# A two-layer transformer trunk on one core: stationary tiles placed at multiples of 512 bytes in SBUF

## The chip, the core and the metric

One core of one Trainium2 chip runs the whole program in one launch. The metric is the device time of that launch in microseconds, median of the runs. Before the change it is 2316.6 us (three runs, 2315.55 to 2317.71).

## What is computed

A trunk of two layers over 256 tokens of width 2048, all in fp32. Each layer is a mixer and a squared-ReLU MLP, each behind an RMS norm and added to the residual stream x. Layer 0's mixer joins eight heads of differential attention and eight heads of a gated delta rule; layer 1's is dilated attention over sixteen heads. Most of the arithmetic is the products with weights:

```python
for l in range(DEPTH):                                   # DEPTH = 2
    if l % 2 == 0:
        x = x + diff_delta_mixer(rms_norm(x, ab_norm[i]), ...)   # h @ w_in [2048 x 7184], ..., o @ w_out [2048 x 2048]
    else:
        x = x + dilated_mixer(rms_norm(x, c_norm[i]), ...)       # h @ w_in [2048 x 6144], ..., o @ w_out [2048 x 2048]
    x = x + jnp.square(jax.nn.relu(rms_norm(x, mlp_norm[l]) @ mlp_w1[l])) @ mlp_w2[l]   # 2048 x 8192, 8192 x 2048
```

## The kernel before, in words

**The large products.** `dense` (line 189) makes a block of at most 512 columns of an activation times a weight matrix, for both 128-token halves, in two PSUM tiles. It goes over the contraction in chunks of 128 rows, mostly 16 of them. To keep fp32's accuracy with the faster fp32r matmuls, both operands are split into a high part and a rest: the weights on the fly (ScalarE casts the high part `wh` at line 201, VectorE subtracts it for the rest `wl` at line 107), the activations when they are made. So a chunk is six matmuls of 512 columns, three for each token half: high by high (line 206), high by rest (207), rest by high (208). The activation is the operand that TensorE loads as stationary (128 x 128 fp32, 512 bytes to a partition), the weights are the moving one. Weights come in pieces of two chunks, 512 KB, through four buffers (`wload`, line 174), issued on SyncE's queue; the split goes through six buffers of `wh` and of `wl`.

In this text an intermediate dense product is called by its PSUM tiles: `b`, `bv`, `z`, `a`, `av` make layer 0's inputs, `wo` its output product, `c`, `cv`, `co` the same for layer 1, `m` the MLP's first product and `n` its second. An MLP runs in four groups (`mlp`, line 294); a group is four denses `m_0` to `m_3`, 512 hidden columns each, and four denses `n_0` to `n_3` that take those 2048 hidden columns as their 16 chunks and add to the four column blocks of x. A dense of 16 chunks has 96 matmuls, so a group's `m` half and its `n` half have 384 each, and the program has 9504 such matmuls of 10,230.

**The stationary tiles.** The normed activations of `b` to `a`, `c` and `m` are `xa`, `xb`, `xc`, `xd` (with h or l for the part), in the pool `xp`. The MLP's hidden activations are `hh` and `hl` (in the trace `m_0hh` to `m_3hl`, by their dense), six buffers each in the pools `hp0` and `hp1`. The mixers' outputs `oh` and `ol` (`g0oh` to `g3ol` and `d0oh` to `d3ol` in layer 0, `e0oh` to `e7ol` in layer 1) lie in the mixers' pools `mp` and `mq`, between other tiles. Everything else that is loaded as stationary belongs to small fp32 products and transposes of the mixers and norms: 726 matmuls, of which 420 are transposes.

**From one MLP product to the next.** After the last matmul of a dense `m_b`, ScalarE takes it out of PSUM with the ReLU and squares it (`r`, line 123), VectorE transposes it in 16 instructions of 32 partitions (`hT`, line 289), ScalarE casts the high part (`hh`, line 314) and VectorE subtracts for the rest (`hl`, line 107). That is a generator (`spread`) of which `dense` runs a step every second chunk of the following dense, so VectorE's instructions for it stand between the weight splits of that dense. The hidden block of `m_3` is made within `n_0`, which needs it at its chunks 12 to 15.

**Where a tile lies.** A pool's tiles follow one another in SBUF, and pools follow one another in the order in which they are opened: `cp`, `wp`, `xp`, `sp`, and behind `sp` whatever pool is open at the time (`mp`, then `hp0`, then `mq`, then `hp1`, one after the other over the same place). `sp` holds small scratch tiles and sums to 4736 bytes, which is 9 x 512 + 128. So the pools ahead of it begin at multiples of 512, and each pool behind it begins 128 bytes past one. The built program has the stationary tiles of the 9504 matmuls at these places:

| address modulo 512 | matmuls before | tiles | matmuls after |
|---|---|---|---|
| 0 | 6000 | `xa` to `xd`; `e1` to `e7` of `co` | 9504 |
| 128 | 3072 | all hidden tiles of `n` | 0 |
| 160 | 336 | `d0` to `d3`, `g1` to `g3` of `wo` | 0 |
| 64 | 48 | `g0` of `wo` | 0 |
| 320 | 48 | `e0` of `co` | 0 |

The moving tiles `wh` and `wl` lie at multiples of 512 before and after. Of the 726 small ones 218 lie at a multiple of 512 before and 203 after: most move by 128 bytes, so some come onto a multiple and some leave it.

Of the kernel before, what the change touches and what calls it, by code (L numbers as in the profile page):

```python
# [11 lines left out]
F32 = mybir.dt.float32  # L12
F32R = mybir.dt.float32r
# [4 lines left out]
PSUM = bass.MemoryType.PSUM  # L18

P = 128  # L20
# [67 lines left out]
def trunk(  # L88
# [6 lines left out]

    cp = ctx.enter_context(tc.tile_pool(name="cp", bufs=1))
    wp = ctx.enter_context(tc.tile_pool(name="wp", bufs=6))
    xp = ctx.enter_context(tc.tile_pool(name="xp", bufs=4))
    sp = ctx.enter_context(tc.tile_pool(name="sp", bufs=2))
    dp = ctx.enter_context(tc.tile_pool(name="dp", bufs=1, space=bass.MemoryType.DRAM))  # L100
# [3 lines left out]

# [1 line left out]
    def tt(o, a, b, op):  # L106
# [32 lines left out]
    def rsqrt(o, s, n, scale, name, eps=EPS):  # L139
        """o = (s * scale + eps) ** -0.5, by Newton from the exponent's half."""  # L140
        z = sp.tile([P, 16], F32, tag="rs_z", name=name + "z")[:, :n]
        q = sp.tile([P, 16], F32, tag="rs_q", name=name + "q")[:, :n]
        seed = sp.tile([P, 16], I32, tag="rs_i", name=name + "i")[:, :n]
        ts(z, s, scale, eps, ALU.mult, ALU.add)
        ts(seed, z.bitcast(I32), -0.5, RSQRT_MAGIC, ALU.mult, ALU.add)
        r = seed.bitcast(F32)
        for _ in range(3):
            tt(q, r, r, ALU.mult)
            stt(q, q, -0.5, z, ALU.mult, ALU.mult)
            stt(o, q, 1.5, r, ALU.add, ALU.mult)  # L150
            r = o

    # Work that runs between the steps of the large products: streams of generators.
    streams = {"g": deque(), "s": deque(), "o": deque()}
# [14 lines left out]

# [1 line left out]
    def wload(wsrc, k0, nm):  # L171
# [10 lines left out]
    def drip():  # L182
        """Between two row chunks of a large product: a step of a stream or two."""
        step("gs"[tick[0] % 2])
        if tick[0] % 4 == 3:
            step("o")
        tick[0] += 1

    def dense(wsrc, stat, kcs, nm, pre=(), every=1):
        """[T, sum of columns] = stat.T @ w over the 128-row chunks kcs, in PSUM."""  # L190
        n = sum(s.shape[1] for s in wsrc)
        ps = [psd.tile([P, 512], F32, tag="d", name=f"{nm}p{h}") for h in range(NH)]
        first, last = kcs[0], kcs[-1]
        for j, kc in enumerate(kcs):
            if j % 2 == 0:
                raw = pre[j // 2] if j // 2 < len(pre) else wload(wsrc, kc, nm)
            w = raw[:, j % 2, :n]
            wh = wp.tile([P, 512], F32R, tag="wh", name=f"{nm}h{kc}")[:, :n]
            wl = wp.tile([P, 512], F32R, tag="wl", name=f"{nm}l{kc}")[:, :n]
            with tc.high_priority(offset=AHEAD):  # L200
                S.copy(wh, w)  # L201
                tt(wl, w, wh.bitcast(F32), ALU.subtract)
            for h in range(NH):
                sh, sl = stat(kc, h)
                o = ps[h][:, :n]
                E.matmul(o, lhsT=sh, rhs=wh, start=kc == first, stop=False)  # L206
                E.matmul(o, lhsT=sh, rhs=wl, start=False, stop=False)  # L207
                E.matmul(o, lhsT=sl, rhs=wh, start=False, stop=kc == last)  # L208
            if j % every == 0:
                drip()  # L210
        return ps
# [8 lines left out]

# [1 line left out]
    ca = cp.tile([P, NMAIN], F32, name="ca")  # L222
# [34 lines left out]
    def xt_block(xt, n, norm, nm, dst, pool=None):  # L257
        """Block n of x times the norm's gains, transposed and split, in steps; by the vector engine given a pool."""
        if pool is not None:
# [23 lines left out]
    def turn_quadrant(src, dst, i):  # L283
        """dst[d, chunk, tok] = src[tok, half, (chunk, d)] for the tokens on 32 partitions, by 32x32 blocks."""
        q = slice(32 * i, 32 * i + 32)
        sv = src[q].rearrange("p h (c j f) -> p h c j f", c=4, j=4)
        for j in range(4):
            dv = dst[32 * j:32 * j + 32].rearrange("p c (h t) -> p h c t", h=NH)
            V.transpose(out=dv[:, :, :, q], in_=sv[:, :, :, j, :])  # L289

    def next_norm(n, norm, nm, dst, pool=None):
        """After block n of x is final: what the next norm takes from it."""
        stats_block(xs[n], n, nm + "s")
        yield from xt_block(xs[n], n, norm, nm, dst, pool if n < 3 else None)
        if n == 3:
            stats_end(nm + "e")
            yield
# [38 lines left out]

# [1 line left out]
    win = ab_w_in[0]  # L338
# [6 lines left out]

    grow0 = cp.tile([16, P], F32, name="grow0")
    warm = sp.tile([P, 512], F32, tag="junk", name="warm")
# [6 lines left out]
    for n in range(4):  # L354
# [7 lines left out]
        if n < 3:  # L362
            pre.append(wload(b_cols(0), 2 * n, "b0"))
    with ExitStack() as mix:
        mp = mix.enter_context(tc.tile_pool(name="mp", bufs=1))

# [14 lines left out]

        # rope tables with the gains in them: [tok, half, q/k, dim]
        cga = cp.tile([P, NH, 2, 64], F32, name="cga")
# [66 lines left out]

        # gates and bz
        sz = [None] * NH
# [19 lines left out]
        def gates(a, b):  # L472
            ts(beta, b, 0.5, 0.5, ALU.mult, ALU.add)
            ts(nbeta, beta, -1.0, None, ALU.mult)
            tt(a, a, dtb.unsqueeze(1).broadcast_to([P, NH, 8]), ALU.add)
            # softplus(a) = max(a, 0) + log1p(exp(-|a|)), log1p(y) = 2 atanh(y / (2 + y))
            ab = mp.tile([P, NH, 8], F32, name="gab")
# [55 lines left out]
        def conv(raw, rnm, chunks, y, nm):  # L533
            """y[d, 4, T] = silu(causal conv) of four channel chunks."""
            xc = mp.tile([P, 4, T + 4], F32, tag="xc", name=nm + "x")
# [41 lines left out]
        def gdn(qks, s, vb, nm):  # L577
            """Heads 2s, 2s+1 over both 128-token chunks; tiles are [128, (chunk, head), 128]."""
            def mt(tag, n=4, share=None):
# [23 lines left out]
            ts(sq, rs[:, 4:8], 128.0 ** -0.5, None, ALU.mult)  # L603
            # decays
            dd = mt("dd")
# [23 lines left out]
            for i, (h, e) in enumerate(tiles):  # L629
                hd = 2 * s + e  # L630
                stt(m[:, i, :], pk[:, i * P:(i + 1) * P], nbeta[:, h, hd:hd + 1], dd[:, i, :], ALU.mult, ALU.mult)
            # the 16x16 blocks on m's diagonals, one to a partition
            scr, sxy = scm[s % 2], scx[s % 2]
# [12 lines left out]
            yield  # L646
            # (I + M)^-1 of the blocks, from 2x2 up
            xc = mp.tile([32, 2, BLK, BLK], F32, tag="g_P", name=nm + "xc")
# [30 lines left out]
            for i in range(4):  # L679
                for q in range(2):  # L680
# [3 lines left out]
                        xc[i * 8:(i + 1) * 8, q])  # L684
            # X = (I + M)^-1 and its transpose Y, from those blocks up
            xy = mp.tile([P, 2, 4, P], F32, tag="xy", name=nm + "xy")
# [90 lines left out]
        def out_T(o, nm, dst, s, gain):  # L777
            """dst[s]: [d, head, T], split, of o[tok, (chunk, head), d]."""
            t = ps_t(nm + "ot")
            for h in range(NH):  # L780
                for e in range(2):
                    transpose(t[:, e * T + h * P:e * T + h * P + P], o[:, 2 * h + e, :])
            oh = mp.tile([P, 2, T], F32R, tag=f"oh{nm}", name=nm + "oh")
            ol = mp.tile([P, 2, T], F32R, tag=f"ol{nm}", name=nm + "ol")
            act(oh, quads(t, 2), AF.Identity, scale=gain)
            stt(ol, quads(t, 2), gain, oh.bitcast(F32), ALU.mult, ALU.subtract)
            dst[s] = (oh, ol)
# [35 lines left out]
        def rope_mix(r, dim, cg, sg, h, uw):  # L823
            """uw[:, 0] = the gained and rotated 512 columns (q's and k's) of r[:, h]."""
            hd = dim // 2
# [175 lines left out]

# [1 line left out]
    cb = []  # L1003
    with tc.tile_pool(name="hp0", bufs=6) as hp:
        mlp(0, nb, hp, lambda n: streams["s"].append(next_norm(n, 2, f"xc{n}", cb, hp)))

# [1 line left out]
    cin = c_w_in[0]  # L1008
    cstat = stat_of(cb)
    with ExitStack() as mix:  # L1010
        mp1 = mix.enter_context(tc.tile_pool(name="mq", bufs=1))
        oc = [None] * 8
        vcs = [None] * 4

        def c_side(r, s, nm):
# [55 lines left out]
            for e in range(2):  # L1071
# [3 lines left out]
                E.matmul(po[:, e * T + P:(e + 1) * T], lhsT=vs[1], rhs=pT[:, e, T:], start=False, stop=True)  # L1075
            oh = mp1.tile([P, 2, T], F32R, tag=f"oh{nm}", name=nm + "oh")
            ol = mp1.tile([P, 2, T], F32R, tag=f"ol{nm}", name=nm + "ol")
            S.copy(oh, quads(po, 2))
# [50 lines left out]

# [1 line left out]
    ov = out[0].rearrange("(h p) d -> p h d", p=P)  # L1131
# [32 lines left out]
```

## Time and profile before

| | |
|---|---|
| median of three runs | 2316.6 us |
| span of the profiled execution, first to last instruction | 2313.0 us |
| its time beside the span | 3.6 us less than the median of the runs; the page gives no other time of its own |
| TensorE matmul busy | 2298.6 us of the span |
| TensorE weight load busy | 1889.0 us |
| VectorE / ScalarE busy | 1733.1 / 1275.1 us |
| bytes moved | 426.65 MB, mean 184 GB/s |

How to read it: a matmul's record is longer than its share of the engine, since matmuls are pipelined: one of 512 columns is recorded with some 390 ns, and the next starts some 230 ns after it. So TensorE's pace is read from the starts of matmuls, or from the length of a stretch over the matmuls in it. A weight load is a record of its own (PEld) and stands beside the matmul before it.

### The profile page before, as it was taken

How to read it: one execution, taken by the hardware profiler on the slowest of the kernel's cores; microseconds unless marked ns; L12 is line 12 of the kernel's file. 1: busy time of each engine (PE TensorE's matmuls, PEld its weight loads, DVE VectorE, ACT ScalarE, POOL GpSimd, SP SyncE). 2: the span in 40 equal slices, each digit the busy share in tenths (PEclk: the TensorE clock that was granted, in tenths of full speed). 3: DMA queues.
4: the chain of work that ended last, by engine and by line, in shares of the span. 5: the costliest groups of instructions: out<-in, count | busy, mean ns of one | idle time of the engine just before them, and what ended most of it. 6: DMA issues, size and time to landing. Idle time of an engine off the chain costs nothing.

```text
span 2313.0 us, 31488 instructions
## 1 busy us (share of the span) xinstructions
PE 2298.6 (99%) x10536; PEld 1889.0 (82%) x10536; DVE 1733.1 (75%) x3539; ACT 1275.1 (55%) x2376; POOL 5.6 (0%) x15
## 2 busy tenths in 40 slices
PE   9999999999999999999999999999999999999999
PEld 8888888788888888888888888888888888888887
DVE  7758778867757757857898888987875775775774
ACT  6656665655545545545555555556554554554553
POOL 0000000000000000000000000000000000000000
PEclk9999999999999999999999999999999999999999
DMA  8655454556566666665656555555656656656564
GB/s 264 174 170 166 149 174 143 166 180 190 192 188 183 202 186 186 202 188 186 198 183 200 172 166 176 171 175 181 190 193 189 192 191 190 192 191 189 185 209 155
DMA packets 264775, 426.65 MB, mean 184 GB/s; under 512 B 22514, under 2 KB 94372, under 8 KB 264612
## 3 DMA queue, kind: packets, MB, share of 16 engines
q1 hardware_dynamic: 255812, 420.04, 57.7%
q10 hardware_dynamic: 8800, 4.60, 0.8%
q8 instruction: 82, 1.34, 0.2%
q14 instruction: 81, 0.66, 0.1%
HBM read 420.11 MB, written 4.46 MB: 184 GB/s over the span
## 4 chain that ended last, share of the span: by engine, by line
PE 88%; DVE 8%; DMA 2%; ACT 1%; issue 1%; SPq 0%; ACTq 0%; DVEq 0%
PE n_0p L208 3%; PE n_2p L207 3%; PE n_1p L207 3%; PE n_1p L208 3%; PE n_2p L206 3%; PE n_1p L206 3%; PE n_2p L208 3%; PE n_0p L207 3%; PE n_0p L206 3%; PE n_3p L208 3%; PE n_3p L207 3%; PE n_3p L206 3%; PE m_0p L206 3%; PE m_0p L207 3%; PE m_0p L208 3%; PE m_3p L208 3%
## 5 line engine op out<-in xcount | busy, mean ns | idle before, releaser
L107 DVE TENSOR_TENSOR n_3l<-n_3r,n_3h 128x512 fp32r<-128x512 f32 x128 | 88.5, 692 | 73.0 <-ACT n_3h L201 72.6
L107 DVE TENSOR_TENSOR n_2l<-n_2r,n_2h 128x512 fp32r<-128x512 f32 x128 | 88.4, 692 | 73.0 <-ACT n_2h L201 72.6
L107 DVE TENSOR_TENSOR m_0l<-m_0r,m_0h 128x512 fp32r<-128x512 f32 x128 | 88.5, 692 | 68.0 <-ACT m_0h L201 67.8
L201 ACT CAST n_3h<-n_3r 128x512 fp32r<-128x512 f32 x128 | 79.3, 621 | 94.8 <-PE n_3p L208 59.4
L201 ACT CAST n_2h<-n_2r 128x512 fp32r<-128x512 f32 x128 | 79.3, 620 | 94.8 <-PE n_2p L208 59.4
L107 DVE TENSOR_TENSOR n_1l<-n_1r,n_1h 128x512 fp32r<-128x512 f32 x128 | 87.0, 691 | 55.0 <-ACT n_1h L201 54.8
L201 ACT CAST m_0h<-m_0r 128x512 fp32r<-128x512 f32 x128 | 79.6, 622 | 83.8 <-DVE m_0l L107 39.8
L201 ACT CAST n_1h<-n_1r 128x512 fp32r<-128x512 f32 x128 | 78.6, 620 | 81.7 <-PE n_1p L208 59.4
L201 ACT CAST m_1h<-m_1r 128x512 fp32r<-128x512 f32 x128 | 78.1, 622 | 64.7 <-PE m_1p L208 35.3
L107 DVE TENSOR_TENSOR m_1l<-m_1r,m_1h 128x512 fp32r<-128x512 f32 x128 | 87.1, 691 | 33.7 <-ACT m_1h L201 32.0
L201 ACT CAST n_0h<-n_0r 128x512 fp32r<-128x512 f32 x128 | 77.4, 619 | 48.5 <-PE n_0p L208 37.1
L201 ACT CAST m_3h<-m_3r 128x512 fp32r<-128x512 f32 x128 | 77.1, 621 | 46.8 <-PE m_3p L208 35.3
L201 ACT CAST m_2h<-m_2r 128x512 fp32r<-128x512 f32 x128 | 76.9, 621 | 46.8 <-PE m_2p L208 35.3
L107 DVE TENSOR_TENSOR n_0l<-n_0r,n_0h 128x512 fp32r<-128x512 f32 x128 | 84.9, 689 | 11.3 <-ACT n_0h L201 9.6
L107 DVE TENSOR_TENSOR m_3l<-m_3r,m_3h 128x512 fp32r<-128x512 f32 x128 | 84.9, 689 | 11.3 <-ACT m_3h L201 9.6
L107 DVE TENSOR_TENSOR m_2l<-m_2r,m_2h 128x512 fp32r<-128x512 f32 x128 | 84.9, 689 | 11.2 <-ACT m_2h L201 9.5
L289 DVE STREAM_TRANSPOSE m_0hT<-m_0r 32x256 f32<-32x256 f32 x128 | 55.8, 436 | 10.5 <-ACT m_0r L123 8.0
L289 DVE STREAM_TRANSPOSE m_1hT<-m_1r 32x256 f32<-32x256 f32 x128 | 55.8, 436 | 10.4 <-ACT m_1r L123 7.9
L289 DVE STREAM_TRANSPOSE m_2hT<-m_2r 32x256 f32<-32x256 f32 x128 | 55.8, 436 | 10.4 <-ACT m_2r L123 7.9
L289 DVE STREAM_TRANSPOSE m_3hT<-m_3r 32x256 f32<-32x256 f32 x128 | 55.8, 436 | 10.4 <-ACT m_3r L123 7.9
L208 PE MATMUL n_0p<-n_0h,m_3hl 128*128 128x512 f32 x64 | 25.8, 403 | 0.0
L207 PE MATMUL n_0p<-n_0l,m_2hh 128*128 128x512 f32 x64 | 25.3, 396 | 0.0
(2552 smaller groups left out, 7405.7 us busy)
## 6 DMA issues: line engine op xcount, KB each, us to landing
m_0r<-in_mlp_w_dram SPq DMA_DIRECT2D x64, 512.0 KB
m_1r<-in_mlp_w_dram SPq DMA_DIRECT2D x64, 512.0 KB
m_2r<-in_mlp_w_dram SPq DMA_DIRECT2D x64, 512.0 KB
m_3r<-in_mlp_w_dram SPq DMA_DIRECT2D x64, 512.0 KB
n_0r<-in_mlp_w_dram SPq DMA_DIRECT2D x64, 512.0 KB
n_1r<-in_mlp_w_dram SPq DMA_DIRECT2D x64, 512.0 KB
n_2r<-in_mlp_w_dram SPq DMA_DIRECT2D x64, 512.0 KB
n_3r<-in_mlp_w_dram SPq DMA_DIRECT2D x64, 512.0 KB
```

What stands on the lines that cost most here:

```text
L107: V.tensor_tensor(out=o, in0=a, in1=b, op=op)
L201: S.copy(wh, w)
L206: E.matmul(o, lhsT=sh, rhs=wh, start=kc == first, stop=False)
L207: E.matmul(o, lhsT=sh, rhs=wl, start=False, stop=False)
L208: E.matmul(o, lhsT=sl, rhs=wh, start=False, stop=kc == last)
L289: V.transpose(out=dv[:, :, :, q], in_=sv[:, :, :, j, :])
```

## The change

The pool `sp` is opened ahead of `wp`; a tile of 96 fp32 columns (384 bytes) that nothing uses is put in it, and `grow0` (512 bytes) goes from `cp` into `sp`'s rotating buffer `junk`. `sp` then sums to 5120 bytes, ten times 512. `oh` and `ol` get a pool of their own, opened ahead of `mp` and of `mq`; each is 2048 bytes, so the pool is a multiple of 512 too. The diff also takes out comments, which moves line numbers by up to four; nothing else is in it.

```diff
     cp = ctx.enter_context(tc.tile_pool(name="cp", bufs=1))
+    sp = ctx.enter_context(tc.tile_pool(name="sp", bufs=2))
     wp = ctx.enter_context(tc.tile_pool(name="wp", bufs=6))
     xp = ctx.enter_context(tc.tile_pool(name="xp", bufs=4))
-    sp = ctx.enter_context(tc.tile_pool(name="sp", bufs=2))
...
-    grow0 = cp.tile([16, P], F32, name="grow0")
+    grow0 = sp.tile([16, P], F32, tag="junk", name="grow0")
+
+    sp.tile([P, 96], F32, tag="fill", name="fill", bufs=1)
     warm = sp.tile([P, 512], F32, tag="junk", name="warm")
...
     with ExitStack() as mix:
+        op = mix.enter_context(tc.tile_pool(name="op", bufs=1))
         mp = mix.enter_context(tc.tile_pool(name="mp", bufs=1))
...
-            oh = mp.tile([P, 2, T], F32R, tag=f"oh{nm}", name=nm + "oh")
-            ol = mp.tile([P, 2, T], F32R, tag=f"ol{nm}", name=nm + "ol")
+            oh = op.tile([P, 2, T], F32R, tag=f"oh{nm}", name=nm + "oh")
+            ol = op.tile([P, 2, T], F32R, tag=f"ol{nm}", name=nm + "ol")
...
     with ExitStack() as mix:
+        op1 = mix.enter_context(tc.tile_pool(name="oq", bufs=1))
         mp1 = mix.enter_context(tc.tile_pool(name="mq", bufs=1))
...
-            oh = mp1.tile([P, 2, T], F32R, tag=f"oh{nm}", name=nm + "oh")
-            ol = mp1.tile([P, 2, T], F32R, tag=f"ol{nm}", name=nm + "ol")
+            oh = op1.tile([P, 2, T], F32R, tag=f"oh{nm}", name=nm + "oh")
+            ol = op1.tile([P, 2, T], F32R, tag=f"ol{nm}", name=nm + "ol")
```

In the built program every engine has the same instructions in the same order as before, and the same waits, but for ScalarE's first ones, at the program's start (`xas0j` and `xas1j` are scratch that the squares of x go to, on the two buffers of `junk`; DMAHW is a queue of DMA completions). Before:

```order
L125 ACT_TABLE_LOAD [waits DMAHW3_49]
L125 ACTIVATE xas0j_245,ssqp<-xq_100 128x512 [waits DMAHW0_49]
L123 ACTIVATE xa0h<-xa0t_132,gt 128x256 [waits DVE_49,PE_49]
L201 CAST b0h_225<-b0r_108 128x512 [waits DMAHW5_49,DMAHW4_49]
L201 CAST b0h_235<-b0r_108 128x512
L123 ACTIVATE xa0h<-xa0t_132,gt 128x256 [waits DVE_49]
L123 ACTIVATE xa0h<-xa0t_141,gt 128x256 [waits PE_49]
L125 ACTIVATE xas0j_247,ssqp<-xq_100 128x512
```

And with the change:

```order
L125 ACT_TABLE_LOAD [waits DMAHW0_49,DMAHW3_49,DVE_49]
L125 ACTIVATE xas0j_249,ssqp<-xq_101 128x512 [waits PE_49]
L123 ACTIVATE xa0h<-xa0t_136,gt 128x256 [waits DVE_49,PE_49]
L201 CAST b0h_229<-b0r_109 128x512 [waits DMAHW5_49,DMAHW4_49]
L201 CAST b0h_239<-b0r_109 128x512
L123 ACTIVATE xa0h<-xa0t_136,gt 128x256 [waits DVE_49]
L123 ACTIVATE xa0h<-xa0t_145,gt 128x256 [waits PE_49]
L125 ACTIVATE xas0j_251,ssqp<-xq_101 128x512 [waits DMAHW2_49]
```

The two `junk` buffers now hold `grow0` and `warm` first. So the first square waits also for the memset of `warm` (VectorE) and for the warm-up matmuls that read it (TensorE), and the second for the load of `grow0` (DMAHW2).

## Rows read from the trace of the kernel before

**Rows 1.** The page: the span, TensorE's busy time, and its granted clock in 40 slices of the span (9 is 90% or more); from the chain of work that ended last, the shares by engine.

```profile
span 2313.0 us, 31488 instructions
...
PE 2298.6 (99%) x10536; PEld 1889.0 (82%) x10536; DVE 1733.1 (75%) x3539; ACT 1275.1 (55%) x2376; POOL 5.6 (0%) x15
...
PEclk9999999999999999999999999999999999999999
...
PE 88%; DVE 8%; DMA 2%; ACT 1%; issue 1%; SPq 0%; ACTq 0%; DVEq 0%
```

**Rows 2.** Stretches of the two MLPs that hold the eight `n` halves of the groups, each from the first start of its matmuls to the first start of the next half (the last one to the start of its last matmul): start and end, length, TensorE busy, granted clock, DMA share, GB/s. First and last of eight, and their sum and mean.

```profile
597.48:687.08 89.60, 89.60 (x386) 1.00 0.61 193
...
2219.52:2308.91 89.39, 89.39 (x385) 1.00 0.56 182
sum 715.73, PE 715.73; mean PE 89.47
```

**Rows 3.** The same view of the `m` halves, six of them (the first of each MLP also holds transposes of the norm and is left out).

```profile
687.08:774.16 87.08, 87.08 (x385) 1.00 0.62 189
...
2132.44:2219.52 87.08, 87.08 (x385) 1.00 0.60 188
sum 522.42, PE 522.42; mean PE 87.07
```

**Rows 4.** The same view of single denses: `n_0` and `n_1` of a group (96 matmuls each), the `m_0` that follows them, the first dense of the second part of `wo` (48 matmuls), and that of `co` (36 matmuls).

```profile
774.16:796.55 22.39, 22.39 (x98) 1.00 0.60 195
796.55:818.85 22.30, 22.30 (x97) 1.00 0.63 200
...
863.47:885.25 21.78, 21.78 (x98) 1.00 0.62 192
461.95:473.13 11.18, 11.18 (x50) 1.00 0.57 187
1565.85:1574.01 8.16, 8.16 (x38) 1.00 0.62 192
```

**Rows 5.** The timeline of TensorE (start, length, line, out<-in) in the first dense of `co`: the first matmul on the tiles of `e0` (at 320), of `e1`, of `e2` and of `e3` (at 0); 12 matmuls lie between one and the next.

```profile
1507.68 0.39 PE L206 MATMUL co00p<-co00h,e0oh 128*128 128x512 f32 x1
...
1510.48 0.40 PE L206 MATMUL co00p<-co00h,e1oh 128*128 128x512 f32 x1
...
1513.23 0.39 PE L206 MATMUL co00p<-co00h,e2oh 128*128 128x512 f32 x1
...
1515.95 0.39 PE L206 MATMUL co00p<-co00h,e3oh 128*128 128x512 f32 x1
```

**Rows 6.** Who TensorE's weight loads waited for, over the span (waited for: us in total, times, longest): the first row of that answer.

```profile
PEld n_0p L208 <- DVE m_3hl L107: 1.9, 8, 0.2
```

**Rows 7.** The timeline around that wait in one `n_0`, by engine: ScalarE's square of `m_3` and VectorE's first and last work on it (in brackets the idle time before, and who ended it), then TensorE's first matmul of this dense, and those on both sides of the first load of `m_3hl`.

```profile
775.60 1.06 ACT L123 ACTIVATE m_3r<-m_3r 128x1024 f32<-128x1024 f32 x1
...
776.69 0.88 DVE L289 STREAM_TRANSPOSE m_3hT<-m_3r 32x256 f32<-32x256 f32 x2 [0.98 <-ACT m_3r L123]
...
790.05 1.23 DVE L107 TENSOR_TENSOR m_3hl<-m_3hT,m_3hh 128x1024 fp32r<-128x1024 f32 x1 [0.40 <-ACT m_3hh L314]
...
774.16 0.40 PE L206 MATMUL n_0p<-n_0h,m_0hh 128*128 128x512 f32 x1
...
791.33 0.19 PEld L208 LDWEIGHTS n_0p<-n_0h,m_3hl 128*128 128x128 f32 x1 [0.23 <-DVE m_3hl L107]
791.37 0.46 PE L208 MATMUL n_0p<-n_0h,m_3hl 128*128 128x512 f32 x1
...
791.67 0.39 PE L206 MATMUL n_0p<-n_0h,m_3hh 128*128 128x512 f32 x1
```

**Rows 8.** The same timeline: four transposes in a row each, of tiles at 0 (`b2raw`), 448 (`g1xy`) and 320 (`d0o`) modulo 512.

```profile
224.79 0.60 PE L231 MATMUL c2t<-ca,b2raw 128*128 128x128 f32 x4
226.61 0.60 PE L231 MATMUL g1lx<-ca,g1xy 128*128 128x128 f32 x4
...
235.77 0.60 PE L231 MATMUL d0ot<-ca,d0o 128*128 128x128 f32 x4
```

**Rows 9.** VectorE's transposes at line 289 (min/median/max ns, first and last start): from and into tiles of the pool `hp0` and `hp1` (at 128 modulo 512), and into tiles of `mq` at 192 and at 384.

```profile
L289 DVE STREAM_TRANSPOSE m_3hT<-m_3r x128: 432/436/442, 600.0 to 2233.8; 32x256 f32<-32x256 f32 x128
...
L289 DVE STREAM_TRANSPOSE e0qkT<-e0qk x16: 427/436/442, 1253.1 to 1264.3; 32x256 f32<-32x256 f32 x16
L289 DVE STREAM_TRANSPOSE e1qkT<-e1qk x16: 428/435/441, 1300.0 to 1311.2; 32x256 f32<-32x256 f32 x16
```

**Rows 10.** The timeline of the program's start.

```profile
0.91 0.48 DVE L348 MEMSET warm<- 128x512 f32 x1 [0.91 <-PEq L1150]
...
1.45 3.78 PE L351 MATMUL pw<-warm 128*128 128x128 f32 x16 [1.45 <-DVE warm L348]
...
5.16 0.28 PE L231 MATMUL pg<-ca,grow 16*128 16x16 f32 x1
...
5.50 1.28 ACT L125 ACT_TABLE_LOAD   x1 [5.50 <-DMA xq<-in_x_dram]
6.79 0.63 ACT L125 ACTIVATE xas0j<-xq 128x512 f32<-128x512 f32 x1
```

**Rows 11.** Who the issue of weight loads on SyncE's queue waited for, over the span: us in total, times, longest.

```profile
SPq L176 <- DVE m_1l L107: 170.8, 64, 3.3
SPq L176 <- DVE n_0l L107: 145.5, 64, 3.3
```

## The prediction

> **What bounds the kernel now.** First the page: TensorE is busy in 2298.6 of 2313.0 us, its granted clock reads nine in all 40 slices (full speed, 2.4 GHz), and 88% of the chain that ended last is TensorE's [rows 1]. So a nanosecond off each of the 9504 large matmuls reaches the end, unless another engine then becomes late. Second, TensorE's pace stage by stage, as length over matmuls. The `n` halves of the MLPs take 715.73 us for 3071 steps from one matmul's start to the next, 233.1 ns a step [rows 2]; the `m` halves take 522.42 us for 6 x 384, 226.75 ns [rows 3]. Both stream 512 columns of weights against 128 stationary columns, in the same order of six, at the same clock. What differs is where the stationary tile lies: 0 modulo 512 in `m`, 128 in `n`.
>
> Third, a place where one dense mixes the two, which takes the stage's other work out of the comparison. In the first dense of `co`, 12 matmuls on `e0` (at 320) take 2.80 us, the next 12 on `e1` (at 0) 2.75, the next 12 on `e2` (at 0) 2.72 [rows 5]: 233, 229 and 227 ns. So the pace changes with the tile's place, and settles within about a dozen matmuls. `wo` and `co` side by side say the same: 11.18 us for 48 matmuls on tiles at 160 are 232.9 ns, 8.16 us for 36 at 0 are 226.7 [rows 4]. Residues of 128, 160 and 320 cost alike, some 6.2 ns a matmul.
>
> Fourth, whether TensorE is alone at the end of its chain in `n`. In `n_1` to `n_3` it is. In `n_0` it is not: all eight times, the load of `m_3hl` waits for VectorE [rows 6], 0.24 us each. In the `n_0` of [rows 7], which begins at 774.16, VectorE starts on `m_3` at 776.69, when ScalarE's square is done, and ends at 791.28, with a single idle of 0.40 us on the way; the load starts at 791.33. The reader should see that this strip of 14.6 us begins with the end of `m_3` and not with anything that `n_0` does, and that it already ends last: the matmuls on both sides of that load stand 0.30 us apart, 0.07 more than a step.
>
> **The change part by part.** No instruction is added, removed or moved, on no queue; addresses change, and three waits at the start.
>
> *`n`, 3072 matmuls from 128 to 0.* At the pace of `m`, 3071 steps take 696.3 us, not 715.7: 19.4 us less. From that comes what `n_0` can't give. Its chunk 12 asks for `m_3hl` after 74 matmuls, which at 226.75 ns is 16.78 us after its start; VectorE has it at 17.12 as before, so the load starts at 17.17 and the matmul behind it at 17.51, as before [rows 7]. Only the 21 steps left run faster: 17.51 + 21 x 0.22675 = 22.27 us, against 22.39 before [rows 4] and 21.77 at the full pace. So each `n_0` keeps 0.50 us of its possible saving, 4.0 us over eight. After that pause the pace has to settle again; priced by `e1`, 12 x 2.3 ns = 0.03 us, eight times: 0.2. Left: 19.4 - 4.0 - 0.2 = **15.2 us**, 14.4 of it in the 24 denses `n_1` to `n_3`.
>
> *`wo`, 384 matmuls from 64 and 160 to 0.* The second part's 192 run by themselves or beside a few transposes: 192 x 6.2 ns = 1.2 us. Between the first part's 192 stand small fp32 products, and behind such a break the pace settles first; by `e1`'s 229 ns they give 4 ns each, 0.8 us. Bounds: none at all in the first part, if the mixer's chain holds it (1.2), and 6.2 ns for all 384 (2.4). I take **2.0**.
>
> *`co`, 48 matmuls on `e0`, and the settling of `e1` behind them:* 48 x 6.2 ns less what settles anyway, **0.3 us**.
>
> *The 726 small stationary tiles.* Fifteen more of them lie off a multiple than before, and most of the others only change their residue. Four transposes take 0.60 us at residue 0, at 448 and at 320 alike [rows 8], so this is 0. If each of the tiles that leave a multiple cost the 6.2 ns (at most all 218), it would be 1.4 us; that is the bound on this side.
>
> *The three waits at the start.* The memset of `warm` ends at 1.39 us, the warm-up matmuls at 5.23, and the transpose that reads `grow0` starts at 5.16, so its load had landed. ScalarE begins at 5.50, waiting for x, and its first square starts at 6.79 behind the table load [rows 10]. Every new wait is over before the old one; 0 us. If they were not hidden, the cost would be the distance of these times, under 1 us.
>
> *Other engines on the moved tiles.* VectorE's transposes take 436 ns into tiles at 128, at 192 and at 384 [rows 9]; I take 0 for 128 to 0. *The loads of weights.* A faster `n` asks for a 512 KB piece every 12 x 226.75 ns = 2.72 us; the `m` halves do so already, and SyncE's loads there wait for a free buffer, up to 3.3 us each, not TensorE for them [rows 11]. 0 us.
>
> The sum is 15.2 + 2.0 + 0.3 = 17.5 us. The profiled span would go from 2313.0 to 2295.5 us. That span is 3.6 us below the median of the runs, which I leave as it is: 2316.6 - 17.5 = **2299.1 us**.
>
> **The rivals.** *The full gain.* VectorE's strip in `n_0` could end earlier, if something in it hangs on TensorE's pace (the casts it takes from ScalarE wait for buffers that TensorE frees). For it: that dependence exists. Against it: VectorE has one idle of 0.40 us, and that for ScalarE's cast of its own transposes [rows 7]. It would give the 4.2 us back: 2294.9 us.
>
> *A part of `n_1` to `n_3` is held by something not seen in `m`,* for instance the second product's weights, read by another stride. Against it: the loads of `n_0` wait for buffers as those of `m` do [rows 11]. With half of the 14.4 us lost: 2306.3 us.
>
> *No change.* The place of the tile might not matter, and `n` differ from `m` by something else that goes with the stage. `e0` against `e2` in one dense speaks against that [rows 5]. It would leave 2316.6 us. Two rules would lead there. The Trainium skill, "TensorE: Matmul & The Clock Gate", step 1 of Part 2, has the next tile's weight load run behind the matmul in flight, on a read port of its own; so a load slower by some nanoseconds would be hidden behind 512 columns, for which that page's gap is an estimated 216 ns. By that rule the sum is 0; the trace does not agree, since steps of 227 and 233 ns differ by the stationary tile alone. And the Trainium skill, "SBUF — State Buffer", Specifications, gives lines of 16 bytes as what a read should not straddle; all residues here are multiples of 16, so that rule, too, sees nothing to gain, and rows 5 speak against it in the same way.
>
> *Slower, by VectorE.* Its strip between `m_3` and `m_3hl` ends last in every `n_0`, so whatever lengthens it is paid eight times, one for one. The change moves the tiles that it reads and writes (`r`, `hT`, `hl`). If their new place were worse for VectorE, a strip longer by 2.2 us (15%) would use up the 17.5 us, and one longer by 2.8 us (19%) make the kernel measurably slower; by 25%, 8 x 3.65 = 29.2 us, it is 2328 us. Against it stand the equal 436 ns at three residues [rows 9].
>
> **How the numbers follow.** About 0.2% (4.6 us) is what a measurement of this kernel can tell from no change. Forecast 0.65; full gain 0.12; partly held 0.15; no change 0.05; slower by VectorE 0.03. The first three are faster by over 0.2%: 0.92. The range begins just under the full gain with `wo` at its upper bound (2294.9 - 0.4) and reaches up to where about two thirds of `n_1` to `n_3` still gain and `wo`'s and the small tiles' bounds go against it, without quite taking in the half: 2294.5 to 2305.0, with some 0.8 inside.
>
> **What would show it.** In the new profile the `n` halves should take 22.27 + 3 x 21.77 = 87.6 us each (89.5 now), and `m` 87.1 as before; `n_0` should be longer than `n_1` by 0.5 us, and the wait of `m_3hl`'s load grow from 1.9 to 8 x (0.24 + 0.43), some 5.3 us. `wo`'s first dense of the second part should take 10.9 us. If `n_0` comes out at 21.8, the strip was not what holds it; if `n_1` stays at 22.3, the place of the tile was not the cause; and if VectorE's transposes are no longer 436 ns, the last rival is at work.

## The result, and the profile after

The changed kernel takes **2300.6 us** (median of five runs, 2298.86 to 2301.77) against 2316.6 (five runs, 2315.55 to 2318.15): a ratio of 0.9927, with a 95% interval of 0.9915 to 0.9939, or 16.0 us less. Forecast were 2299.1 us, and 2294.5 to 2305.0.

The page of the profiled execution, to be held against [rows 1]: span, busy times, granted clock by slice, and the chain's shares.

```profile
span 2299.3 us, 31489 instructions
...
PE 2280.7 (99%) x10536; PEld 1889.1 (82%) x10536; DVE 1732.9 (75%) x3539; ACT 1275.7 (55%) x2376; POOL 5.6 (0%) x15
...
PEclk9999999999999999999999999999999999999999
...
PE 84%; DVE 10%; ACT 2%; issue 2%; DMA 1%; ACTq 0%; SPq 0%; DVEq 0%
```

TensorE's busy time fell by 17.9 us; VectorE, ScalarE and the weight loads are where they were. So TensorE's work became shorter and no other engine's did. Where, tell the stretches: first the `n` halves (first and last of eight, and their sum), as in [rows 2]. A row gives start and end, length, the busy time (and the number of instructions) of TensorE, its weight loads, VectorE, ScalarE and GpSimd, then the granted clock, the DMA share and GB/s.

```profile
599.67:687.25 87.58, 87.34 (x385) 72.01 (x384) 55.30 (x88) 42.22 (x68) 0.00 (x0) 1.00 0.64 198
...
2207.89:2295.24 87.35, 87.10 (x384) 71.81 (x383) 52.27 (x84) 39.09 (x63) 0.00 (x0) 1.00 0.60 187
sum 700.39, PE 698.48 PEld 575.88 DVE 463.33 ACT 342.05 POOL 0.00; mean PE 87.31 PEld 71.98 DVE 57.92 ACT 42.76 POOL 0.00
```

The `m` halves, as in [rows 3]:

```profile
687.25:774.29 87.04, 87.04 (x386) 72.10 (x384) 68.14 (x118) 48.65 (x77) 0.00 (x0) 1.00 0.63 188
...
2120.85:2207.89 87.04, 87.04 (x386) 72.10 (x384) 68.15 (x118) 48.33 (x77) 0.00 (x0) 1.00 0.63 187
sum 522.24, PE 522.24 PEld 432.53 DVE 408.87 ACT 291.54 POOL 0.00; mean PE 87.04 PEld 72.09 DVE 68.15 ACT 48.59 POOL 0.00
```

And the single denses of [rows 4]: `n_0`, `n_1`, the `m_0` behind them, `wo`'s first dense of the second part, `co`'s.

```profile
774.29:796.59 22.30, 22.05 (x98) 17.94 (x96) 18.75 (x34) 12.26 (x20) 0.00 (x0) 1.00 0.59 196
796.59:818.35 21.76, 21.76 (x98) 18.02 (x96) 12.18 (x19) 9.98 (x16) 0.00 (x0) 1.00 0.66 208
861.87:883.63 21.76, 21.76 (x98) 18.02 (x96) 12.18 (x19) 10.46 (x17) 0.00 (x0) 1.00 0.64 193
465.18:476.06 10.88, 10.88 (x50) 9.01 (x48) 6.64 (x11) 4.99 (x8) 0.00 (x0) 1.00 0.61 193
1560.39:1568.55 8.16, 8.16 (x37) 6.76 (x36) 5.26 (x9) 3.75 (x6) 0.00 (x0) 1.00 0.62 193
```

The `n` halves are 715.73 - 700.39 = 15.34 us shorter, the six `m` halves 0.2 us (presumably because a dense behind an `n` no longer has to settle). `n_1` now takes exactly what `m_0` takes; `n_0` alone takes 0.54 us more. By the starts of their matmuls (a dense is taken from its first matmul to the next matmul behind its last), the eight denses of `wo` went from 112.19 to 110.70 us, the eight of `co` from 93.21 to 92.85, and all the others of layer 1's mixer stayed (287.79 and 287.81). In sum 15.3 + 1.5 + 0.4 + 0.2 = 17.4 us.

What is left over has the other sign: the two profiled spans differ by 13.7 us, not 17.4. In the profile after, `b0`, the first dense, begins 0.5 us later and takes 27.62 us where it took 25.58, and layer 0 from `z2` to `wo` takes 1.2 us more. The experiments come back to this.

The first dense of `co`, as in [rows 5]: the first matmul on each of four tiles.

```profile
1502.58 0.39 PE L206 MATMUL co00p<-co00h,e0oh 128*128 128x512 f32 x1
...
1505.30 0.39 PE L206 MATMUL co00p<-co00h,e1oh 128*128 128x512 f32 x1
...
1508.02 0.39 PE L206 MATMUL co00p<-co00h,e2oh 128*128 128x512 f32 x1
...
1510.74 0.39 PE L206 MATMUL co00p<-co00h,e3oh 128*128 128x512 f32 x1
```

Three times 2.72 us: `e0` is as fast as `e2`, and `e1` has nothing to settle. Then the wait of [rows 6], and the timeline of [rows 7], in the `n_0` that begins at 774.29:

```profile
PEld n_0p L208 <- DVE m_3hl L107: 5.3, 8, 0.7
```

```profile
775.73 1.06 ACT L123 ACTIVATE m_3r<-m_3r 128x1024 f32<-128x1024 f32 x1
...
776.83 0.88 DVE L289 STREAM_TRANSPOSE m_3hT<-m_3r 32x256 f32<-32x256 f32 x2 [0.99 <-ACT m_3r L123]
...
790.19 1.23 DVE L107 TENSOR_TENSOR m_3hl<-m_3hT,m_3hh 128x1024 fp32r<-128x1024 f32 x1 [0.40 <-ACT m_3hh L314]
...
774.29 0.39 PE L206 MATMUL n_0p<-n_0h,m_0hh 128*128 128x512 f32 x1
...
791.47 0.19 PEld L208 LDWEIGHTS n_0p<-n_0h,m_3hl 128*128 128x128 f32 x1 [0.67 <-DVE m_3hl L107]
791.47 0.50 PE L208 MATMUL n_0p<-n_0h,m_3hl 128*128 128x512 f32 x1 [0.25 <-DVE m_3hl L107]
```

The strip from the end of the square to `m_3hl` is 14.6 us long, as before; the load asks sooner and so waits 0.67 us where it waited 0.23. VectorE's transposes, [rows 9], and SyncE's waits for buffers, [rows 11]:

```profile
L289 DVE STREAM_TRANSPOSE m_3hT<-m_3r x128: 432/436/442, 602.2 to 2222.2; 32x256 f32<-32x256 f32 x128
```

```profile
SPq L176 <- DVE m_1l L107: 170.8, 64, 3.3
```

Both are unchanged.

### The profile page after: what moved, and what is told of

Read it like the earlier page. It is cut to its first block, busy times and chain, and to the rows that moved or that the text cites. A ratio compares the mean times of both kernels' runs of the same rounds, so it can differ in the third digit from the quotient of the medians.

```text
span 2299.3 us, 31489 instructions
## 1 busy us (share of the span) xinstructions
PE 2280.7 (99%) x10536; PEld 1889.1 (82%) x10536; DVE 1732.9 (75%) x3539; ACT 1275.7 (55%) x2376; POOL 5.6 (0%) x15
## 4 chain that ended last, share of the span: by engine, by line
PE 84%; DVE 10%; ACT 2%; issue 2%; DMA 1%; ACTq 0%; SPq 0%; DVEq 0%
PE m_0p L208 3%; PE m_0p L206 3%; PE m_1p L208 3%; PE m_2p L208 3%; PE n_1p L208 3%; PE n_2p L208 3%; PE m_0p L207 3%; PE n_2p L207 3%; PE n_2p L206 3%; PE n_1p L207 3%; PE m_2p L207 3%; PE m_1p L206 3%; PE m_2p L206 3%; PE n_1p L206 3%; PE m_1p L207 3%; PE n_3p L208 3%
## 5 line engine op out<-in xcount | busy, mean ns | idle before, releaser
L206 PE MATMUL n_0p<-n_0h,m_3hh 128*128 128x512 f32 x64 | 25.0, 390 | 0.0
```

## The experiments

The theory to be tested, P: a matmul is slower by some 6 ns when the tile that is loaded lies off a multiple of 512, whatever the stage. Its rivals: S, stage `n` has something of its own; W, what counts is something in which the weights' place has a part too. For `n_0`: V, VectorE's strip holds it; its rival, something else does.

**The change again.** No edit.

> The changed kernel once more, unaltered, as the yardstick of this set: 2300.6 us, within 2298.5 to 2302. Its second use: in the first profile of the change, the stretch up to layer 0 took 2.2 us longer than in the kernel before (the granted clock fell back to half for 6.8 us at 8.3 us), and layer 0 up to wo 1.2 us longer. If these belong to the change, they stand here again, with the first matmul of the first m half at 511.6 us. If they vary from run to run, that matmul starts anywhere between 508 and 512 us, while the n halves stay at 87.58 us and wo's first dense of the second part at 10.88.

Measured: 2297.95 us, on a chip where the kernel before took 2315.3; the ratio is 0.9930 (0.9914 to 0.9947). The `n` halves took 87.56 to 87.60 us, `wo`'s dense 10.88. The first `m` half began at 507.7 us, not 511.6: `b0` took 25.24 us and layer 0 as long as in the kernel before. So the 3.7 us that the first profile lost at the start and in layer 0 vary from run to run of one kernel; in this profile, span 2295.2, the difference is 17.8 us.

**Only the half of the change that moves `n`.**

```diff
-        op = mix.enter_context(tc.tile_pool(name="op", bufs=1))
...
-            oh = op.tile([P, 2, T], F32R, tag=f"oh{nm}", name=nm + "oh")
+            oh = mp.tile([P, 2, T], F32R, tag=f"oh{nm}", name=nm + "oh")
```

(likewise `ol`, and both in layer 1)

> One part of the change alone: the pool sp is moved and filled up (n at 0), but the heads' output tiles oh and ol stay in the mixers' own pools, whose other tiles put them at 32 and 448 in wo and at 384 and 192 in co. Place of the tile: n halves 87.58 us as in the change; wo as before the change (11.2 us for its first dense of the second part), and co, where 336 of 384 matmuls stood at 0 in both kernels, pays 6.2 ns for all 384: its denses of 36 matmuls take 8.38 us and not 8.16. In all 2300.6 + 1.5 to 2.0 (wo) + 2.4 (co) = 2304.5 to 2305.0 us. Rival, wo and co differed for another reason than the place (what runs beside them): co stays at 8.16 and the total at 2300.6 to 2302.6.

Measured: 2301.38 us (2300.35 to 2301.75), 3.4 more than the change, ratio to before 0.9941 (0.9926 to 0.9956). `n` as in the change (87.56 and 87.58 us). The eight denses of `co` together take 94.49 us, 1.6 more, and those of `wo` 112.01, 1.3 more; `wo`'s first dense of the second part, with its tiles at 32, takes 11.20 us as before the change. The dense of [rows 4] in `co`:

```profile
1559.90:1568.26 8.36, 8.36 (x37) 6.78 (x36) 5.26 (x9) 3.72 (x6) 0.00 (x0) 1.00 0.64 187
```

8.36 us for what took 8.16 in both kernels, with nothing changed but the residue (0 to 384). The kind was right, and the size below the expectation (2301.38 for 2304.5 at the least): this dense pays 5.7 ns a matmul, and the denses of `co` with transposes between their matmuls less, so that the breaks seem to hide a part.

**All stationary tiles at 128; then the weights alone at 128.** The first puts 128 bytes ahead of `xp`; the second takes the filler tile out, so that `wp` begins at 128, and puts 384 bytes behind it.

```diff
+    pd = ctx.enter_context(tc.tile_pool(name="pd", bufs=1))
+    pd.tile([P, 32], F32, name="pad")
     xp = ctx.enter_context(tc.tile_pool(name="xp", bufs=4))
```

```diff
     wp = ctx.enter_context(tc.tile_pool(name="wp", bufs=6))
+    pd = ctx.enter_context(tc.tile_pool(name="pd", bufs=1))
+    pd.tile([P, 96], F32, name="pad")
     xp = ctx.enter_context(tc.tile_pool(name="xp", bufs=4))
...
-    sp.tile([P, 96], F32, tag="fill", name="fill", bufs=1)
```

> The change, with 128 bytes put ahead of the pools, so that all 9504 stationary tiles lie at 128 and all weights stay at 0. Place of the tile, whatever the stage: every step 233 ns; 9504 x 6.2 ns = 58.9 us, less 4.0 that n_0 loses to VectorE anyway and some 2 in layer 0, where breaks between the matmuls hide it: 2353 us, within 2345 to 2357; m halves 89.5 us and not 87.1, n halves 89.5, co's denses of 36 matmuls 8.38. Rival, stage n alone is sensitive: only n gets slower, 2315.8 us, with m at 87.1.

> The change, but with all weights (wr, wh, wl), which stream as moving data, put at 128 and the stationary tiles kept at 0. If only the stationary tile's place counts, the time is the change's, 2300.6 us, steps of 226.7 ns. Rival, the moving data's place counts as well or instead, at the same 6.2 ns: 2353 us as with all stationary tiles off; at half of that, 2327.

Measured: 2341.03 us with the tiles at 128 (ratio to before 1.0113, 1.0093 to 1.0133) and **2342.69 us with the weights at 128** (1.0119, 1.0104 to 1.0134). One `m` half and the `n` half behind it, with the tiles off:

```profile
692.83:782.06 89.23, 89.23 (x386) 72.34 (x384) 68.41 (x118) 48.77 (x77) 0.00 (x0) 1.00 0.62 185
782.06:871.36 89.30, 89.30 (x386) 72.27 (x385) 55.31 (x88) 42.09 (x68) 0.00 (x0) 1.00 0.61 192
```

and with the weights off:

```profile
694.34:783.57 89.23, 89.23 (x385) 72.35 (x384) 68.40 (x118) 48.79 (x77) 0.00 (x0) 1.00 0.62 184
783.57:873.15 89.58, 89.58 (x385) 72.04 (x384) 55.30 (x88) 42.08 (x68) 0.00 (x0) 1.00 0.61 193
```

S has fallen: `m` is as slow as `n` when its tiles are off. P has fallen too, as far as it speaks of the stationary tile alone: the weights' place costs the same. W is left. (The 12 us by which the first stayed under its expectation lie in the mixers: the MLPs lost 33 us of the 34 that 6144 x 6.2 ns, less `n_0`'s 4, give; the 3360 other matmuls lost 10 and not 19, presumably because breaks stand between many of them.)

**Both off, alike and unlike.** The pool `pd` of 128 bytes goes ahead of `wp`, which moves weights and tiles alike; in a second kernel 128 bytes more go ahead of `xp`; in a third 256.

```diff
     sp = ctx.enter_context(tc.tile_pool(name="sp", bufs=2))
+    pe = ctx.enter_context(tc.tile_pool(name="pe", bufs=1))
+    pe.tile([P, 32], F32, name="pad2")
     wp = ctx.enter_context(tc.tile_pool(name="wp", bufs=6))
+    pd = ctx.enter_context(tc.tile_pool(name="pd", bufs=1))
+    pd.tile([P, 32], F32, name="pad")
     xp = ctx.enter_context(tc.tile_pool(name="xp", bufs=4))
```

> The change with the stationary tiles and the weights both put at 128, after either alone had cost the same (2341.0 us with the stationary tiles at 128, 2342.7 with the weights there, against 2298.0; steps of some 232.7 ns against 226.7). Theory A, each read that is not at a multiple of 512 pays for itself: steps of 239 ns, 2298.0 + 43.1 + 44.7 = 2386 us. Theory B, a step pays once, whichever of the two is off: 232.7 ns, 2341 to 2343 us. Theory C, what counts is that both have the same residue, not that it is 0: steps of 226.7 ns, 2298 to 2300 us.

> As before, but the stationary tiles at 256 and the weights at 128, so that both are off and the two differ. Theory A (each pays): 239 ns, 2386 us. Theory B (once): 232.7 ns, 2341 to 2343 us. Theory C (the two residues' difference): 232.7 ns, 2341 to 2343 us. So it tells A from B and C, and with the run before all three apart.

> The change with the stationary tiles at 384 and the weights at 128: neither at a multiple of 256, but 256 apart. What has been seen: 0 against 0, 128 against 128 and 256 against 0 run at 226.7 ns a step; 128 against 0, 0 against 128, 256 against 128 and 64 against 0 at some 232.6. If only the distance of the two, modulo 256, counts: 226.7 ns, the change's own time, 2298 to 2300 us. If instead the two must be equal or both at multiples of 256: 232.6 ns, 2339 to 2343 us.

Measured: tiles and weights both at 128, **2298.43 us** (0.992, 0.990 to 0.994); tiles at 256 and weights at 128, **2339.04** (1.0095, 1.0075 to 1.0115); tiles at 384 and weights at 128, **2300.51** (0.993, 0.9912 to 0.9948). An `m` and an `n` half of each, in that order:

```profile
684.25:771.29 87.04, 87.04 (x386) 72.07 (x384) 68.12 (x118) 48.64 (x77) 0.00 (x0) 1.00 0.62 188
771.29:858.85 87.56, 87.33 (x386) 72.00 (x384) 55.26 (x88) 42.20 (x68) 0.00 (x0) 1.00 0.61 198
```

```profile
691.59:780.83 89.24, 89.24 (x386) 72.35 (x385) 68.40 (x118) 48.82 (x77) 0.00 (x0) 1.00 0.61 185
780.83:870.13 89.30, 89.30 (x386) 72.26 (x384) 55.29 (x88) 42.05 (x68) 0.00 (x0) 1.00 0.61 193
```

```profile
686.98:774.02 87.04, 87.04 (x386) 72.07 (x385) 68.12 (x118) 48.68 (x77) 0.00 (x0) 1.00 0.64 188
774.02:861.60 87.58, 87.36 (x386) 71.99 (x385) 55.28 (x88) 42.20 (x68) 0.00 (x0) 1.00 0.62 198
```

Theory C holds in all three: what counts is the distance of the stationary tile's place from that of the weights, modulo 256. In the first and the third kernel no tile and no weight lies at a multiple of 256, and the pace is that of the change: 87.04 us for an `m` half, 87.56 and 87.58 for an `n` half.

**Two more distances.** A pad as the first tile of `hp0` and of `hp1`.

```diff
     with tc.tile_pool(name="hp0", bufs=6) as hp:
+        hp.tile([P, 64], F32, tag="pad", name="pad0", bufs=1)
...
     with tc.tile_pool(name="hp1", bufs=6) as hp:
+        hp.tile([P, 16], F32, tag="pad", name="pad1", bufs=1)
```

> The change, with the stationary tiles of the first MLP's n halves at 256 and of the second's at 64, all others at 0. If any place off a multiple of 512 costs the same, as 32, 160, 320 and 384 did, both MLPs' n halves take 89.4 to 89.6 us (87.6 in the change) and the total is 2298.0 + 8 x 1.9 = 2313 us. Rival, a multiple of 256 is good enough: the first MLP's n halves stay at 87.6 and the second's are 89.5, 2305.6 us. Rival, the cost grows with the residue: 64 below 256, the halves 88.1 and 89.5, about 2307.

Measured: 2307.68 us in one run; the second `n` half of each MLP:

```profile
772.64:860.25 87.61, 87.38 (x386) 72.00 (x385) 55.27 (x88) 42.20 (x68) 0.00 (x0) 1.00 0.61 198
...
1859.04:1948.65 89.61, 89.61 (x385) 72.11 (x384) 55.42 (x88) 42.12 (x68) 0.00 (x0) 1.00 0.60 194
```

256 is free, 64 costs in full: the rival that 256 is good enough, which C needs. With the weights at 0, tiles at 32, 64, 128 and 384 have now cost some 6 ns a matmul, 160 and 320 too [rows 4, 5], and 0 and 256 nothing.

**Only the low parts off, or only the high parts.** A pad between `hh` and `hl` in `hp0`, and ahead of `hh` in `hp1`.

```diff
+            if layer == 1:
+                hp.tile([P, 32], F32, tag="pa", name=nm + "pa", bufs=1)
             hh = hp.tile([P, 4, T], F32R, tag="hh", name=nm + "hh")
+            hp.tile([P, 32 if layer == 0 else 96], F32, tag="pb", name=nm + "pb", bufs=1)
             hl = hp.tile([P, 4, T], F32R, tag="hl", name=nm + "hl")
```

> The change, with only a part of the stationary tiles of the n halves moved off: in the first MLP the low parts hl at 128 and the high parts hh at 0, in the second the high parts at 128 and the low ones at 0; all weights at 0. A step of three matmuls is hh on wh, hh on wl, hl on wh. In the first MLP one load of three is off, in the second two. If each load off pays for itself, the n halves take 87.6 + 0.6 = 88.2 us in the first MLP and 88.9 in the second, 2298.0 + 4 x 0.65 + 4 x 1.3 = 2305.8 us. If a load pays in the matmul that streams while it runs, the longer step in the first MLP is the second of three (hh on wl, in whose shadow hl is loaded), at about 232.6 against 226.7; if a matmul pays for its own tile, it is the third (hl on wh). Rival, any tile off costs all steps alike: the halves 89.5 us in both MLPs, 2313 us.

Measured: 2314.61 us in one run; the second `n` half of each MLP:

```profile
775.52:864.45 88.93, 88.93 (x386) 72.55 (x384) 55.35 (x88) 42.05 (x68) 0.00 (x0) 1.00 0.63 195
...
1866.02:1955.62 89.60, 89.60 (x385) 72.06 (x384) 55.30 (x88) 42.24 (x68) 0.00 (x0) 1.00 0.62 193
```

None of the theories gave this. Two matmuls of `n_1` in the first MLP, hh on wl and hl on wh, and the loads that start with them (the lines give 0.01 us, too coarse for the lengths, but they show what is loaded while what streams):

```profile
800.20 0.40 PE L207 MATMUL n_1p<-n_1l,m_0hh 128*128 128x512 f32 x1
800.43 0.40 PE L208 MATMUL n_1p<-n_1h,m_0hl 128*128 128x512 f32 x1
...
800.20 0.19 PEld L208 LDWEIGHTS n_1p<-n_1h,m_0hl 128*128 128x128 f32 x1
800.43 0.19 PEld L206 LDWEIGHTS n_1p<-n_1h,m_0hh 128*128 128x128 f32 x1
```

From one matmul's start to the next, averaged over the 384 of each line in `n_1` to `n_3` of the first MLP (in `n_0` the wait for `m_3hl` comes in), hh on wh takes 226.7 ns, hh on wl 232.5, hl on wh 234.2. The second streams while the low part is loaded; the third works on the low part, and the high part that is loaded meanwhile is at distance 0. So one load off costs two matmuls, the one in whose shadow it runs and its own. With the high parts off all three are slow (232.5, 232.5, 235.0), which the same reading gives. It was formed after the run, on one kernel, and why the matmul behind pays as well is open.

**VectorE's strip moved up.** `m_3`'s transposes and its split get precedence over the weight splits around them.

```diff
-        def spread(r, nm, hb):
+        def spread(r, nm, hb, late):
...
-                turn_quadrant(r, hT, i)
+                with tc.high_priority(offset=46 if late else 0):
+                    turn_quadrant(r, hT, i)
...
-            S.copy(hh, hT)
-            tt(hl, hT, hh.bitcast(F32), ALU.subtract)
+            with tc.high_priority(offset=46 if late else 0):
+                S.copy(hh, hT)
+                tt(hl, hT, hh.bitcast(F32), ALU.subtract)
...
-                streams["s"].append(spread(r, nm, hb))
+                streams["s"].append(spread(r, nm, hb, b == 3))
```

> The change, with VectorE's transposes of m_3 and the split behind them given precedence over the weight splits of n_0, so that its strip from m_3 to m_3hl ends earlier. No work is added or left out. In the change m_3hl came 0.4 us too late for n_0's chunk 12, and n_0 took 22.29 us instead of 21.76. If that strip alone holds n_0, it ends about 15.5 us after the start of n_0 and the load asks at 16.78: n_0 takes 21.8, the wait on VectorE goes, and the total falls by up to 8 x 0.53 = 4.2 us, from 2298.0 to 2294 us on this chip. Rival, the delayed weight splits hold the next denses in its place: n_0 at 21.8 but n_1 or a wait for wh or wl longer by as much, 2298. Rival, n_0 is held by something else than VectorE (PSUM, ScalarE's casts): n_0 stays at 22.3, 2298.

Measured: 2294.75 us (2292.63 to 2296.63), ratio to before 0.9901 (0.9884 to 0.9917). `n_0` and `n_1` of one group; the split that makes `m_3hl`; the load that needs it:

```profile
773.69:795.45 21.76, 21.76 (x97) 18.02 (x96) 18.55 (x34) 12.19 (x20) 0.00 (x0) 1.00 0.58 186
795.45:817.21 21.76, 21.76 (x97) 18.02 (x96) 12.14 (x19) 9.98 (x16) 0.00 (x0) 1.00 0.66 221
```

```profile
788.35 1.22 DVE L107 TENSOR_TENSOR m_3hl<-m_3hT,m_3hh 128x1024 fp32r<-128x1024 f32 x1
...
790.24 0.19 PEld L208 LDWEIGHTS n_0p<-n_0h,m_3hl 128*128 128x128 f32 x1
```

The split ends 15.9 us after the start of `n_0`, the load comes at 16.55 and waits for nothing; the row of that wait is gone, and none for a load of an `m` or `n` dense has come in its place. All eight `n_0` take 21.76 us. V is right, and its price was 0.54 us a time (22.30 less 21.76).

**The strip moved up, and the start bridged.** Six matmuls of 128 columns on the zeroed tile go behind the first transposes of x. Beside it ran the unaltered change.

```diff
+            if n == 0:
+                for _ in range(6):
+                    E.matmul(pw[:, :P], lhsT=warm[:, :P], rhs=warm[:, :P], start=True, stop=True)
```

> The change with two things more: the precedence of m_3's transposes and split as in the run on VectorE's strip (n_0 at 21.76 us), and six idle matmuls of 128 columns on the zeroed tile behind the first transposes at the start, where TensorE else waits up to 2.3 us for the first cast. [...] If the idle matmuls keep the clock up, it is 1.00 from 5 to 16 us, b0 starts the layers no later than 32.6 us, and the time is the lower end of the strip's run, 2292 to 2293.5 us. If they only delay the first dense, b0's end is 34 us or later and the time 2294 to 2296.

> The changed kernel again, unaltered, on the chip of this set, as the yardstick of the run before: 2298 to 2301 us, 0.992 to 0.993 of the kernel before; n halves 87.57 us; b0 25 or 27 us as the clock goes.

Measured on one chip: **2293.86 us** (2293.09 to 2294.48) against 2299.65 (2298.70 to 2301.33) for the change; ratios to before 0.9901 (0.9888 to 0.9915) and 0.9928 (0.9914 to 0.9941). The start with the idle matmuls:

```profile
5.00:8.00 3.00, 2.73 (x23) 2.41 (x21) 0.18 (x1) 1.60 (x2) 0.00 (x0) 1.00 0.97 312
8.00:12.00 4.00, 2.85 (x15) 1.94 (x14) 3.01 (x6) 4.00 (x12) 0.00 (x0) 1.00 1.04 350
```

and in the profile of the run before, without them:

```profile
5.00:8.00 3.00, 1.34 (x9) 0.87 (x9) 0.17 (x1) 2.33 (x5) 0.00 (x0) 1.00 0.83 254
8.00:12.00 4.00, 3.40 (x9) 2.58 (x10) 2.78 (x6) 3.57 (x11) 0.00 (x0) 0.50 1.03 347
```

The clock (the third number from the end) stays at its upper level, 2.4 GHz, where it had fallen to 1.2. `b0` takes 25.0 us and not 27.6, but begins 0.7 us later, behind the idle matmuls: its end, 32.9 us after the first warm-up matmul (32.6 in the kernel before, 34.8 in the run of the strip alone), lies between the two expectations (32.6 and 34), and so does the median.

That the idle matmuls held the clock, this one profile doesn't show: in 4 of the 13 profiles without them it stayed up as well. The mean granted clock of every run says more: 1.0 in the four runs here, 0.998 or 0.999 in the five of the change on the same chip. But of the strip alone the two runs that kept 1.0 by themselves took 2292.63 and 2293.82 us, no longer than these four. The median is 0.9 us under that of the strip alone, on another chip and inside its runs' scatter, so a gain in time by the bridge is not shown. The version beats both kernels, for the most part by the strip: of the 5.8 us between it and the change beside it, the `n` halves give 4.2.

## Why the prediction was right, and where it wasn't

*`n`.* Right in its parts: 87.6 us a half was forecast and 87.58 measured, `n_0` 22.27 and 22.30, `n_1` 21.77 and 21.76, the wait of `m_3hl` 5.3 us and 5.3; in sum 15.2 and 15.3. The place at which this was decided is [rows 7]: the strip began with the end of `m_3`, so it could be taken as a fixed 17.1 us after the start of `n_0`, and a faster TensorE would only reach the wait sooner. The strip's run showed the other side of that: with the strip out of the way the 4.2 us come. (One reading of [rows 7] was off, without weight for the sum: the two matmuls 0.30 us apart are the one that uses the load and the next one, so both stand behind the load and not on both sides of it.)

*`wo`, `co`.* 2.0 was forecast for `wo` and 1.5 measured: 1.0 in the second part, where 1.2 had been taken, and 0.5 in the first, where it was 0.8. `co` 0.3 and 0.4. (The window of `wo` in [rows 4] begins 0.02 us late; by its starts that dense took 11.20 us before, 233.3 ns a matmul and not 232.9.)

*Nothing for the small tiles, the start, the other engines and the DMA.* Other engines: the equal 436 ns and busy times. Small tiles: the denses of layer 1's mixer other than `co`, with the transposes among them, took 287.81 us for 287.79. The new waits at the start can't be seen, since the start of one kernel varies by more than their price.

*The sum.* The terms come to 17.4 us by the rows against 17.5; the medians differ by 16.0, 17.4 and 16.6 in the three sets. The 0.8 us in the mean are less than the start alone varies (the first `m` half begins between 507.7 and 511.6 us in three profiles of the change). The time of a run goes with its mean granted clock: in each of the three sets the runs of the change order by it, from 2297.04 us at 1.0 to 2301.77 at 0.998. Whether the change has a part in how the clock goes at the start can't be told, with one profile of the kernel before.

*The cause.* Here the text claimed too much. It named the stationary tile's place modulo 512 as the cause; the rows showed only that tiles at 0 are faster than tiles elsewhere, all with the weights at 0. The runs showed that the distance to the weights counts, modulo 256. The number was right because the weights stay at 0 and no tile of the kernel before lies at 256, so that in this change the two readings agree; with the weights alone moved to 128, the prediction's reading gives 2300.6 us where 2342.69 were measured. No row of the kernel before could have told them apart: none of its large matmuls has its weights off.

*The rules.* The Trainium skill, "TensorE: Matmul & The Clock Gate", Part 2, step ④, gives TensorE two independent read ports into SBUF, one for the streaming operand and one for the loaded one. The runs don't agree, if independent means that the place of one operand can't change what the other costs: with the tiles at 128 the kernel took 2341 us beside weights at 0, and 2298 beside weights at 128. Whether it is the ports that the two share, or something behind them, no run here shows.

*The rivals.* Full gain: `n_0` stayed at 22.30 us. No change: S was shut out by moving `m`. A part of `n_1` to `n_3` held: they took 21.76 us, the pace of `m`. Slower by VectorE: its transposes stayed at 436 ns.

## What to carry to other kernels

Where matmuls load a new fp32 tile of 128 columns each and stream 512, compare the addresses of the loaded and of the streamed tiles: here a distance that is no multiple of 256 cost 2.5 to 3% of every step, and pads of some hundred bytes took it away. The weights were tried at 0 and at 128 only, and all in one kernel. Before such a gain is booked, look for the strip of another engine that ends just in time; it gives the gain back until its order is changed too. And a cause that was read from tiles of which only one side varied is half a cause: move the other side once.

## What the runs showed of the hardware that was not expected

- A matmul of 512 fp32r columns with a new 128-column load in its shadow takes 226.7 ns from start to start where the two operands are a multiple of 256 bytes apart, and 232.4 to 233.4, in the mean of a half, where they aren't (tile/weights 128/0, 0/128, 256/128, 64/0). Off, the single steps alternate, 229 and 238 ns in many stretches, and a dense `n_1` of 96 takes either some 22.31 or 22.40 us.
- The weight load's own record doesn't show it: 188 ns in either case.
- One load off slows two matmuls, so a third of the loads off cost 88.93 - 87.58 = 1.35 us of the 2.0 that all of them cost in an `n` half.
- At the start the granted clock fell from 2.4 to 1.2 GHz in some executions of a kernel and not in others (in 9 of the 13 profiles without the idle matmuls), 8 to 9 us in, after TensorE had waited for x and the first cast; `b0` then took 26.3 to 27.6 us and not 25.0 to 25.6.
